# A skewness kernel: another assignment of rows to partitions, a direct store, other load widths and a later split of the closing sums

## Chip, core and metric

The kernel runs on one core of a Trainium2 chip. The metric is the device time of one execution in microseconds (us), as the median of several runs. Each run has a state: slow, if it is over 1.5% above the fastest of the same kernel, else fast. Ratios are the mean time of one kernel's fast runs over that of the other's fast runs of the same rounds, so they are not quite the ratio of the medians that are quoted beside them.

## The reference, cut to what matters

```python
rows, cols = 1024, 8192                      # x is float32, 33.55 MB
mean = np.mean(x, axis=-1, keepdims=True)
std = np.std(x, axis=-1, keepdims=True)
z = (x - mean) / (std + 1e-8)
return np.mean(z ** 3, axis=-1)              # one number for each row
```

With m1, m2, m3 as the means of x, x² and x³ of a row, var = m2 - m1², and the result is (m3 - 3 m1 (var + m1²/3)) · var^(-1.5). So one pass over x is enough, and no order of columns or rows matters to the sums.

## The kernel before

The rows are taken in 8 blocks of 128, one row for each partition. A block comes in by several loads, each a range of columns (a unit). On each unit ScalarE squares and sums, VectorE multiplies the square by x and sums, and TensorE accumulates transposes, which later give m1.

```python
UNITS = [[512, 1024, 2560, 4096], [4096, 4096], [4096, 4096], [4352, 3840],
         [3328, 2816, 2048], [2048] * 4, [1792, 1792, 1664, 1536, 1408],
         [1152, 1152, 1152, 1152, 1024, 896, 896, 512, 256]]     # layout shortened
xv = x.rearrange("(b p) c -> b p c", p=P)
ob = out.rearrange("(b p) -> b p", p=P)
# ...
for k, w in enumerate(widths):
    xt = xpool.tile([P, w], FP, tag="x", name=f"x_{b}_{k}")
    nc.sync.dma_start(out=xt, in_=xv[b, :, c0 : c0 + w])
    c0 += w
    for s, e in _slices(w):
        # ...
        nc.scalar.activation(out=sq, in_=xt[:, s:e], func=AF.Square, scale=s_scale, accum_out=a2)
        nc.vector.scalar_tensor_tensor(out=cube, in0=sq, scalar=1.0, in1=xt[:, s:e],
                                       op0=ALU.mult, op1=ALU.mult, accum_out=a3)
    # ... transposes of xt into tp on TensorE
# ... blocks 0 to 6 closed together, then block 7:
nc.vector.tensor_scalar(out=m3, in0=v3, scalar1=nm1, scalar2=m3, op0=ALU.mult, op1=ALU.add)
nc.vector.tensor_tensor(out=skew[:, L:NB], in0=m3, in1=rr, op=ALU.mult)
nc.tensor.matmul(out=skT_ps, lhsT=skew, rhs=ident, start=True, stop=True, is_transpose=True)
nc.vector.tensor_copy(out=skT, in_=skT_ps)
nc.sync.dma_start(out=ob, in_=skT)
```

Partition p of block b holds row 128b+p. Written with p = 8e+i that is row 128b+8e+i.

## Time and profile before

| what | value | from |
|---|---|---|
| time | 93.59 us, median of 3 runs (93.39 to 94.45) | the runs |
| span of the profiled run | 91.36 us | the trace |
| first packet of a load, last landing | 1.75 us, 84.93 us | the trace's packet and landing records |
| a packet of 16384 B, of 8192 B (median) | 611 ns, 312 ns | the packet records |
| VectorE, ScalarE, TensorE busy | 81%, 76%, 74% | the page |

A packet here is one row's part of one unit: the 5 loads of 16384 B per row show 640 packets, so 128 a load, 8 for each of its 16 landings. The landing records have one time for each engine's share of a load, and a unit is used when the last of the 16 is there (the first unit's is at 3.69 us, ScalarE's first square of it at 3.78). The page's lines, the waits and the timeline are shown and read in the prediction.

### The profile page before, as it was taken

How to read it: one execution, taken by the hardware profiler on the slowest of the kernel's cores; microseconds unless marked ns; L12 is line 12 of the kernel's file. 1: busy time of each engine (PE TensorE's matmuls, PEld its weight loads, DVE VectorE, ACT ScalarE, POOL GpSimd, SP SyncE). 2: the span in 40 equal slices, each digit the busy share in tenths (PEclk: the TensorE clock that was granted, in tenths of full speed). 3: DMA queues.
4: the chain of work that ended last, by engine and by line, in shares of the span. 5: the costliest groups of instructions: out<-in, count | busy, mean ns of one | idle time of the engine just before them, and what ended most of it. 6: DMA issues, size and time to landing. Idle time of an engine off the chain costs nothing. (4 is left out here: it accounts for less than half of the span.)

```text
span 91.4 us, 1437 instructions
## 1 busy us (share of the span) xinstructions
PE 68.0 (74%) x529; PEld 60.6 (66%) x529; DVE 73.9 (81%) x91; ACT 69.1 (76%) x101; POOL 9.4 (10%) x14
## 2 busy tenths in 40 slices
PE   0391898879495949688889897857789798989610
PEld 0360897779494939587879796747678687867500
DVE  0052290898989798978999999998899999999960
ACT  6350927969595959689889999766798899999830
POOL 3000000000000000000000000000000000699820
PEclk9999999999999999999999999999999999999995
DMA  1999999999999999999999999999999999991000
GB/s 43 362 374 440 445 438 409 430 452 430 402 423 452 442 417 434 435 424 399 430 414 404 430 420 420 423 407 422 419 409 423 406 418 408 406 344 74 0 0 2
DMA packets 4486, 33.64 MB, mean 368 GB/s; under 512 B 504, under 2 KB 640, under 8 KB 2560
## 3 DMA queue, kind: packets, MB, share of 16 engines
q1 hardware_dynamic: 4480, 33.56, 88.6%
q8 instruction: 4, 0.07, 0.3%
q14 instruction: 2, 0.02, 0.0%
HBM read 33.55 MB, written 0.00 MB: 367 GB/s over the span
## 5 line engine op out<-in xcount | busy, mean ns | idle before, releaser
L139 DVE SCALAR_TENSOR_TENSOR sq<-sq,x 128x2048 f32<-128x2048 f32 (+11 forms) x39 | 71.5, 1885 | 13.9 <-ACT sq L135 13.9
L145 PE MATMUL tp<-ident,x 128*128 128x128 f32 x512 | 65.2, 285 | 15.3 <-DMA x<-in_x_dram 15.0
L135 ACT ACTIVATE sq<-x 128x2048 f32<-128x2048 f32 (+12 forms) x41 | 62.8, 1534 | 17.4 <-DMA x<-in_x_dram 15.9
L145 PEld LDWEIGHTS tp<-ident,x 128*128 128x128 f32 x512 | 58.7, 147 | 20.5 <-DMA x<-in_x_dram 16.6
L106 POOL TENSOR_TENSOR vara<-m2a,m1sqa 128x7 f32<-128x7 f32 x1 | 1.3, 1294 | 77.1 <-DVE m3a L97 77.1
L135 ACT ACTIVATION_READ_ACCUMULATOR sq<-x 128x1 f32 x41 | 7.6, 186 | 0.0
L116 PEld LDWEIGHTS s1ps<-onesn,tsb 128*128 128x128 f32 x16 | 2.4, 188 | 5.6 <-ACT tsb L115 5.6
L116 PE MATMUL s1ps<-onesn,tsb 128*128 128x1 f32 x16 | 3.1, 260 | 3.7 <-ACT tsb L115 3.7
L139 DVE DVE_READ_ACCUMULATOR sq<-sq,x 128x1 f32 x39 | 3.2, 83 | 0.0
L110 POOL TENSOR_TENSOR rra<-vara,expo 128x7 f32<-128x7 f32 x1 | 2.6, 2624 | 0.0
L115 ACT COPY tsb<-tp 128x128 f32<-128x128 f32 x8 | 2.0, 249 | 0.0
L72 ACT ACT_TABLE_LOAD x1 | 1.3, 1283 | 0.7 <-PEq L190 0.7
L172 PE MATMUL skT_ps<-ident,skew 128*8 128x128 f32 x1 | 0.3, 273 | 2.0 <-DVE skew L169 2.0
L172 PEld LDWEIGHTS skT_ps<-ident,skew 128*8 128x8 f32 x1 | 0.1, 83 | 2.1 <-DVE skew L169 2.1
L107 POOL TENSOR_TENSOR m1sq3a<-m1sq3a,vara 128x7 f32<-128x7 f32 x1 | 1.2, 1202 | 0.1
L139 DVE SCALAR_TENSOR_TENSOR cubes<-sq,x 128x512 f32<-128x512 f32 (+1 forms) x2 | 1.1, 554 | 0.1
L108 POOL TENSOR_TENSOR m1sq3a<-m1sq3a,nm1a 128x7 f32<-128x7 f32 x1 | 1.1, 1150 | 0.0
L109 POOL TENSOR_TENSOR m3a<-m3a,m1sq3a 128x7 f32<-128x7 f32 x1 | 0.9, 935 | 0.1
L111 POOL TENSOR_TENSOR skew<-m3a,rra 128x7 f32<-128x7 f32 x1 | 0.9, 933 | 0.1
L70 DVE MEMSET onesn<- 128x1 f32 x1 | 0.1, 59 | 0.8 <-PEq L190 0.8
L163 POOL TENSOR_TENSOR rrl<-varl,expo 128x1 f32<-128x1 f32 x1 | 0.6, 562 | 0.6 <-ACT varl L161 0.6
L174 DVE COPY skT<-skT_ps 8x128 f32<-8x128 f32 x1 | 0.3, 278 | 0.4 <-PE skT_ps L172 0.4
(25 smaller groups left out, 4.4 us busy)
## 6 DMA issues: line engine op xcount, KB each, us to landing
x<-in_x_dram SPq DMA_DIRECT2D x5, 2048.0 KB, 18.7
x<-in_x_dram SPq DMA_DIRECT2D x5, 1024.0 KB, 24.2
x<-in_x_dram SPq DMA_DIRECT2D x4, 576.0 KB, 9.8
x<-in_x_dram SPq DMA_DIRECT2D x1, 2176.0 KB, 33.8
x<-in_x_dram SPq DMA_DIRECT2D x1, 1920.0 KB, 36.2
x<-in_x_dram SPq DMA_DIRECT2D x2, 896.0 KB, 15.8
x<-in_x_dram SPq DMA_DIRECT2D x1, 1664.0 KB, 33.9
x<-in_x_dram SPq DMA_DIRECT2D x1, 1408.0 KB, 30.3
```

Source lines behind the costliest of these rows:

```text
L72: nc.scalar.activation(out=tiny, in_=onesn, func=AF.Square)
L106: g.tensor_tensor(out=var, in0=m2, in1=m1sq, op=ALU.subtract)
L107: g.tensor_tensor(out=m1sq3, in0=m1sq3, in1=var, op=ALU.add)
L108: g.tensor_tensor(out=m1sq3, in0=m1sq3, in1=nm1, op=ALU.mult)
L109: g.tensor_tensor(out=m3, in0=m3, in1=m1sq3, op=ALU.add)
L110: g.tensor_tensor(out=rr, in0=var, in1=expo, op=ALU.pow)
L111: g.tensor_tensor(out=skew[:, 0:L], in0=m3, in1=rr, op=ALU.mult)
L115: nc.scalar.copy(out=tsb, in_=tp)
L116: nc.tensor.matmul(out=s1ps[:, b : b + 1], lhsT=tsb, rhs=onesn, start=True, stop=True)
L135: nc.scalar.activation(out=sq, in_=xt[:, s:e], func=AF.Square, scale=s_scale, accum_out=a2)
L139: nc.vector.scalar_tensor_tensor(out=cube, in0=sq, scalar=1.0, in1=xt[:, s:e], op0=ALU.mult, op1=ALU.mult, accum_out=a3,)
L145: nc.tensor.matmul(out=tp, lhsT=xt[:, c * P : (c + 1) * P], rhs=ident, start=(k == 0 and c == 0), stop=(c0 == C and c == n - 1), is_transp ...
```

## The change

Its intent: to shorten the time after the last landing. If partition 8e+i holds rows 128i+8e+b for b from 0 to 7, its 8 results lie side by side in the output, and the finished tile can be stored directly, without a transpose and a copy. The m1 term of the last two blocks becomes one more column of the third sums, so that one reduction adds it. Larger first and last units mean fewer loads. The core of the diff (cut):

```diff
 UNITS = [
-    [512, 1024, 2560, 4096],
-    ...
-    [1152, 1152, 1152, 1152, 1024, 896, 896, 512, 256],
+    [4096, 4096],
+    [4096, 4096],
+    [4096, 4096],
+    [4096, 4096],
+    [3584, 2304, 2304],
+    [2304, 2304, 2048, 1536],
+    [1664, 1792, 1920, 1664, 1152],
+    [1024, 1024, 1152, 1280, 1408, 1152, 1152],
 ]
+S1_ACT = {(0, 0): 1024, (1, 0): 1024, (2, 0): 1024}   # column sums on ScalarE, not TensorE
+EARLY = 6                                             # blocks 0 to 5 closed early
...
-    xv = x.rearrange("(b p) c -> b p c", p=P)
-    ob = out.rearrange("(b p) -> b p", p=P)
+    I = P // ENGINES                                  # ENGINES = 16, I = 8
+    xv = x.rearrange("(i e b) c -> b e i c", i=I, e=ENGINES, b=NB)
+    ov = out.rearrange("(i e b) -> e i b", i=I, e=ENGINES, b=NB)
...
-            nc.sync.dma_start(out=xt, in_=xv[b, :, c0 : c0 + w])
+            nc.sync.dma_start(out=xt, in_=xv[b, :, :, c0 : c0 + w])
...
+        yield act(out=s3u[:, b * K + K - 1 : b * K + K], in_=v3, func=AF.Identity, scale=nm1)
...
-    nc.vector.tensor_scalar(out=m3, in0=v3, scalar1=nm1, scalar2=m3, ...)
-    nc.tensor.matmul(out=skT_ps, lhsT=skew, rhs=ident, ..., is_transpose=True)
-    nc.vector.tensor_copy(out=skT, in_=skT_ps)
-    nc.sync.dma_start(out=ob, in_=skT)
+    nc.vector.tensor_reduce(out=num, in_=s3u[:, F * K :]..., axis=X_AXIS, op=ALU.add)
+    nc.vector.tensor_tensor(out=skew[:, F:NB], in0=num, in1=rr, op=ALU.mult)
+    nc.sync.dma_start(out=ov, in_=skew)
```

More of the change, by code (lines that the diff above doesn't have):

```diff
@@ L15 @@
 UNITS = [
-    [512, 1024, 2560, 4096],
     [4096, 4096],
     [4096, 4096],
-    [4352, 3840],
-    [3328, 2816, 2048],
-    [2048, 2048, 2048, 2048],
-    [1792, 1792, 1664, 1536, 1408],
-    [1152, 1152, 1152, 1152, 1024, 896, 896, 512, 256],
+    [4096, 4096],
[4 more added lines that the diff above has]
+    [1024, 1024, 1152, 1280, 1408, 1152, 1152],
 ]
+S1_ACT = {(0, 0): 1024, (1, 0): 1024, (2, 0): 1024}
 SUB_MAX = 2304
@@ L27 @@
 SQ_BUFS = 4
-PSUM_SQ = 2
+EARLY = 6
+ENGINES = 16
 def _slices(w):
@@ L48 @@
     L = NB - 1
+    F = EARLY
     inv_n = 1.0 / float(C)
@@ L52 @@
     assert len(UNITS) == NB and all(sum(u) == C for u in UNITS)
-    xv = x.rearrange("(b p) c -> b p c", p=P)
-    ob = out.rearrange("(b p) -> b p", p=P)
-    n_sub = [sum(len(_slices(w)) for w in u) for u in UNITS]
-    MAXC = max(n_sub[:L])
-    NL = n_sub[L]
+    nw = len(S1_ACT)
+    assert sorted(b for b, _ in S1_ACT) == list(range(nw)) and nw <= F
+    I = P // ENGINES
+    xv = x.rearrange("(i e b) c -> b e i c", i=I, e=ENGINES, b=NB)
+    ov = out.rearrange("(i e b) -> e i b", i=I, e=ENGINES, b=NB)
+    K = max(sum(len(_slices(w)) for w in u) for u in UNITS) + 1
     xpool = ctx.enter_context(tc.tile_pool(name="xp", bufs=X_BUFS))
@@ L65, with small @@
     psum = ctx.enter_context(tc.tile_pool(name="ps", bufs=2, space=bass.MemoryType.PSUM))
-    psq = ctx.enter_context(tc.tile_pool(name="psq", bufs=2, space=bass.MemoryType.PSUM))
     psum1 = ctx.enter_context(tc.tile_pool(name="ps1", bufs=1, space=bass.MemoryType.PSUM))
-    onesn = onep.tile([P, 1], FP, tag="onesn")
+    def small(name, n):
+        return onep.tile([P, n], FP, tag=name, name=name)
+    onesn = small("onesn", 1)
     nc.vector.memset(onesn, inv_n)
-    tiny = onep.tile([P, 1], FP, tag="tiny")
+    tiny = small("tiny", 1)
@@ L72 @@
     nc.scalar.activation(out=tiny, in_=onesn, func=AF.Square)
-    ident = onep.tile([P, P], FP, tag="ident")
+    ident = small("ident", P)
     make_identity(nc, ident)
-    s2u = onep.tile([P, L * MAXC], FP, tag="s2u")
-    s3u = onep.tile([P, L * MAXC], FP, tag="s3u")
+    s2u = small("s2u", NB * K)
+    s3u = small("s3u", NB * K)
     nc.vector.memset(s2u, 0.0)
     nc.vector.memset(s3u, 0.0)
-    s2l = onep.tile([P, NL], FP, tag="s2l")
-    s3l = onep.tile([P, NL], FP, tag="s3l")
-    cubes = onep.tile([P, 512], FP, tag="cubes")
@@ L82 @@
-    junk = onep.tile([P, NL], FP, tag="junk")
-    expo = onep.tile([P, L], FP, tag="expo")
+    s1a = small("s1a", nw)
+    same = small("same", max(S1_ACT.values()))
+    junk = small("junk", K)
+    expo = small("expo", F)
     nc.gpsimd.memset(expo, -1.5)
-    skew = onep.tile([P, NB], FP, tag="skew")
+    skew = small("skew", NB)
     s1ps = psum1.tile([P, NB], FP, tag="s1ps")
-    Tsb = [onep.tile([P, P], FP, tag=f"tsb{i}", name=f"tsb{i}") for i in range(2)]
-    def small(name, n):
-        return onep.tile([P, n], FP, tag=name, name=name)
@@ L93, in finish_first_blocks, with close_first_blocks @@
-    def finish_first_blocks():
-        m2, m3 = small("m2a", L), small("m3a", L)
+    m1a = small("m1a", F)
+    var2 = small("var2", NB - F)
+    Tsb = [small(f"tsb{i}", P) for i in range(2)]
+    def close_first_blocks():
+        m2, m3 = small("m2a", F), small("m3a", F)
         for dst, src in ((m2, s2u), (m3, s3u)):
             nc.vector.tensor_reduce(
-                out=dst, in_=src.rearrange("p (b c) -> p b c", c=MAXC), axis=X_AXIS, op=ALU.add
-            )
-        m1sq, m1sq3, nm1 = small("m1sqa", L), small("m1sq3a", L), small("nm1a", L)
-        nc.scalar.activation(out=m1sq, in_=s1ps[:, 0:L], func=AF.Square)
-        nc.scalar.activation(out=m1sq3, in_=s1ps[:, 0:L], func=AF.Square, scale=third)
-        nc.scalar.activation(out=nm1, in_=s1ps[:, 0:L], func=AF.Copy, scale=-3.0)
+                out=dst, in_=src[:, 0 : F * K].rearrange("p (b c) -> p b c", c=K),
+                axis=X_AXIS, op=ALU.add,
+            )
+        m1sq, m1sq3, nm1 = small("m1sqa", F), small("m1sq3a", F), small("nm1a", F)
+        nc.scalar.copy(out=m1a[:, nw:F], in_=s1ps[:, nw:F])
+        nc.scalar.activation(out=m1sq, in_=m1a, func=AF.Square)
+        nc.scalar.activation(out=m1sq3, in_=m1a, func=AF.Square, scale=third)
+        nc.scalar.activation(out=nm1, in_=m1a, func=AF.Copy, scale=-3.0)
@@ L104, in finish_first_blocks @@
         g = nc.gpsimd
-        var, rr = small("vara", L), small("rra", L)
+        var, rr = small("vara", F), small("rra", F)
         g.tensor_tensor(out=var, in0=m2, in1=m1sq, op=ALU.subtract)
@@ L110, in finish_first_blocks, with close_on_act @@
         g.tensor_tensor(out=rr, in0=var, in1=expo, op=ALU.pow)
-        g.tensor_tensor(out=skew[:, 0:L], in0=m3, in1=rr, op=ALU.mult)
-    def close_block(b, tp):
-        tsb = Tsb[b % 2]
-        nc.scalar.copy(out=tsb, in_=tp)
-        nc.tensor.matmul(out=s1ps[:, b : b + 1], lhsT=tsb, rhs=onesn, start=True, stop=True)
+        g.tensor_tensor(out=skew[:, 0:F], in0=m3, in1=rr, op=ALU.mult)
+    def close_on_act(b):
+        m2, m1sq, nm1, v3 = (small(f"{t}_{b}", 1) for t in ("m2", "m1sq", "nm1", "v3"))
+        p1 = s1ps[:, b : b + 1]
+        var = var2[:, b - F : b - F + 1]
+        act = nc.scalar.activation
+        yield act(out=junk, in_=s2u[:, b * K : b * K + K], func=AF.Copy, accum_out=m2)
+        yield act(out=m1sq, in_=p1, func=AF.Square)
+        yield act(out=var, in_=m1sq, func=AF.Identity, scale=-1.0, bias=m2)
+        yield act(out=nm1, in_=p1, func=AF.Copy, scale=-3.0)
+        yield act(out=v3, in_=m1sq, func=AF.Identity, scale=1.0 / 3.0, bias=var)
+        yield act(
+            out=s3u[:, b * K + K - 1 : b * K + K], in_=v3, func=AF.Identity, scale=nm1
+        )
@@ L118 @@
+    pending = iter(())
     for b, widths in enumerate(UNITS):
-        last = b == L
         tp = psum.tile([P, P], FP, tag="tp", name=f"tp_{b}")
         c0 = 0
-        j = 0
+        j = b * K
         for k, w in enumerate(widths):
+            last_unit = b == L and k == len(widths) - 1
             xt = xpool.tile([P, w], FP, tag="x", name=f"x_{b}_{k}")
-            nc.sync.dma_start(out=xt, in_=xv[b, :, c0 : c0 + w])
+            nc.sync.dma_start(out=xt, in_=xv[b, :, :, c0 : c0 + w])
@@ L126 @@
             c0 += w
             for s, e in _slices(w):
-                i = b * MAXC + j
-                a2 = s2l[:, j : j + 1] if last else s2u[:, i : i + 1]
-                a3 = s3l[:, j : j + 1] if last else s3u[:, i : i + 1]
-                j += 1
-                in_psum = last and k >= len(widths) - PSUM_SQ
-                pool = psq if in_psum else sqpool
-                sq = pool.tile([P, e - s], FP, tag="sq", name=f"sq_{b}_{k}_{s}")
+                if last_unit:
+                    sq = psum1.tile([P, e - s], FP, tag="sqps", name=f"sqps_{s}")
+                else:
+                    sq = sqpool.tile([P, e - s], FP, tag="sq", name=f"sq_{b}_{k}_{s}")
@@ L135 @@
                 nc.scalar.activation(
-                    out=sq, in_=xt[:, s:e], func=AF.Square, scale=s_scale, accum_out=a2
+                    out=sq, in_=xt[:, s:e], func=AF.Square, scale=s_scale,
+                    accum_out=s2u[:, j : j + 1],
                 )
-                cube = cubes[:, 0 : e - s] if in_psum else sq
+                cube = sqpool.tile([P, e - s], FP, tag="sq", name="cube") if last_unit else sq
                 nc.vector.scalar_tensor_tensor(
                     out=cube, in0=sq, scalar=1.0, in1=xt[:, s:e],
-                    op0=ALU.mult, op1=ALU.mult, accum_out=a3,
+                    op0=ALU.mult, op1=ALU.mult, accum_out=s3u[:, j : j + 1],
@@ L142 @@
                 )
-            n = w // P
+                j += 1
+            w_act = S1_ACT.get((b, k), 0)
+            if w_act:
+                nc.scalar.activation(
+                    out=same[:, 0:w_act], in_=xt[:, w - w_act : w], func=AF.Copy,
+                    scale=inv_n, accum_out=s1a[:, b : b + 1],
+                )
+            n = (w - w_act) // P
             for c in range(n):
@@ L149 @@
                 )
-        close_block(b, tp)
-        if b == L - 1:
-            finish_first_blocks()
-    m2, m3 = small("m2l", 1), small("m3l", 1)
-    nc.scalar.activation(out=junk, in_=s2l, func=AF.Copy, accum_out=m2)
-    nc.vector.tensor_reduce(out=m3, in_=s3l, axis=X_AXIS, op=ALU.add)
-    m1sq, var, nm1, v3 = small("m1sql", 1), small("varl", 1), small("nm1l", 1), small("v3l", 1)
-    p1 = s1ps[:, L:NB]
-    nc.scalar.activation(out=m1sq, in_=p1, func=AF.Square)
-    nc.scalar.activation(out=var, in_=m1sq, func=AF.Identity, scale=-1.0, bias=m2)
-    rr = small("rrl", 1)
-    nc.gpsimd.tensor_tensor(out=rr, in0=var, in1=expo[:, 0:1], op=ALU.pow)
-    nc.scalar.activation(out=nm1, in_=p1, func=AF.Copy, scale=-3.0)
-    nc.scalar.activation(out=v3, in_=m1sq, func=AF.Identity, scale=1.0 / 3.0, bias=var)
-    nc.vector.tensor_scalar(
-        out=m3, in0=v3, scalar1=nm1, scalar2=m3, op0=ALU.mult, op1=ALU.add
-    )
-    nc.vector.tensor_tensor(out=skew[:, L:NB], in0=m3, in1=rr, op=ALU.mult)
-    skT_ps = psum1.tile([NB, P], FP, tag="skT")
-    nc.tensor.matmul(out=skT_ps, lhsT=skew, rhs=ident, start=True, stop=True, is_transpose=True)
-    skT = small("skT", P)[0:NB, :]
-    nc.vector.tensor_copy(out=skT, in_=skT_ps)
-    nc.sync.dma_start(out=ob, in_=skT)
+            if k > 0:
+                next(pending, None)
+                next(pending, None)
+        tsb = Tsb[b % 2]
+        nc.scalar.copy(out=tsb, in_=tp)
+        nc.tensor.matmul(out=s1ps[:, b : b + 1], lhsT=tsb, rhs=onesn, start=True, stop=True)
+        if b == F - 2:
+            nc.vector.tensor_tensor(
+                out=m1a[:, 0:nw], in0=s1ps[:, 0:nw], in1=s1a, op=ALU.add
+            )
+        if b == F - 1:
+            close_first_blocks()
+        if b >= F:
+            pending = close_on_act(b)
+    for _ in pending:
+        pass
+    rr = small("rr2", NB - F)
+    nc.gpsimd.tensor_tensor(out=rr, in0=var2, in1=expo[:, 0 : NB - F], op=ALU.pow)
+    num = small("num2", NB - F)
+    nc.vector.tensor_reduce(
+        out=num, in_=s3u[:, F * K :].rearrange("p (b c) -> p b c", c=K), axis=X_AXIS, op=ALU.add
+    )
+    nc.vector.tensor_tensor(out=skew[:, F:NB], in0=num, in1=rr, op=ALU.mult)
+    nc.sync.dma_start(out=ov, in_=skew)
 _INS = ['x']
```

## The prediction

Marked cuts in it are passages on the hardware that no trace or run here shows; one is the whole argument against the first rival, the 4 MiB pitch. No term of the sum is cut: 84.4 + 3.7 + 2.06 + 0.25 = 90.4 us of span, 92.6 us of time.

> **What bounds the kernel now.** I read the page's head first, for shares and the DMA row.
>
> ```profile
> span 91.4 us, 1437 instructions
> PE 68.0 (74%) x529; PEld 60.6 (66%) x529; DVE 73.9 (81%) x91; ACT 69.1 (76%) x101; POOL 9.4 (10%) x14
> ...
> DMA  1999999999999999999999999999999999991000
> GB/s 43 362 374 440 445 438 409 430 452 430 402 423 452 442 417 434 435 424 399 430 414 404 430 420 420 423 407 422 419 409 423 406 418 408 406 344 74 0 0 2
> ```
>
> No engine is above 81%, but the 16 DMA engines are at 90% or more from the second slice to the 36th, at 400 to 450 GB/s. The load of the 33.55 MB sets the pace, and every engine only follows. Next the waits of all engines, to see who follows whom:
>
> ```profile
> ACT sq L135 <- DMA x<-in_x_dram: 15.9, 16, 3.1
> PE tp L145 <- DMA x<-in_x_dram: 15.0, 18, 3.8
> DVE sq L139 <- ACT sq L135: 13.9, 11, 3.5
> ```
>
> ScalarE and TensorE wait for loads, VectorE for ScalarE's squares. So the time splits in two: the stream until the last column has landed, and the tail after that. The trace's landing records (one time for each engine's share of a load) put the last landing at 84.93 us. Its own packets start at 1.75. The tail is 91.36 - 84.93 = 6.43 us, and the timeline of the end shows what is in it:
>
> ```profile
> 84.53 1.09 DVE L139 SCALAR_TENSOR_TENSOR sq<-sq,x 128x896 f32<-128x896 f32 x1
> ...
> 85.55 1.08 DVE L139 SCALAR_TENSOR_TENSOR sq<-sq,x 128x896 f32<-128x896 f32 x1
> ...
> 86.56 0.68 DVE L139 SCALAR_TENSOR_TENSOR cubes<-sq,x 128x512 f32<-128x512 f32 x1
> ...
> 87.34 0.42 DVE L139 SCALAR_TENSOR_TENSOR cubes<-sq,x 128x256 f32<-128x256 f32 x1
> 87.69 0.08 DVE L139 DVE_READ_ACCUMULATOR cubes<-sq,x 128x1 f32 x1
> 87.81 0.16 DVE L157 TENSOR_REDUCE m3l<-s3l 128x1 f32<-128x9 f32 x1
> 88.09 0.28 DVE L166 TENSOR_SCALAR m3l<-v3l,nm1l,m3l 128x1 f32<-128x1 f32 x1
> 88.47 0.16 DVE L169 TENSOR_TENSOR skew<-m3l,rrl 128x1 f32<-128x1 f32 x1
> 89.00 0.28 DVE L174 COPY skT<-skT_ps 8x128 f32<-8x128 f32 x1 [0.37 <-PE skT_ps L172]
> ```
>
> VectorE still has 2.84 us of cubes to do when the last column lands (87.77 - 84.93): the many small last units did not help, as it works through a queue. Then five small steps, 87.81 to 89.28. The store is issued at 89.30 and 2.06 us later the span ends. ScalarE's line beside it, which matters for what follows:
>
> ```profile
> 85.60 0.37 ACT L135 ACTIVATE sq<-x 128x256 f32<-128x256 f32 x1
> ...
> 86.00 0.24 ACT L115 COPY tsb<-tp 128x128 f32<-128x128 f32 x1
> ...
> 86.72 0.17 ACT L160 ACTIVATE m1sql<-s1ps 128x1 f32<-128x1 f32 x1 [0.27 <-PE s1ps L116]
> ...
> 86.92 0.29 ACT L161 ACTIVATE varl<-m1sql,m2l 128x1 f32<-128x1 f32 x1
> 87.25 0.29 ACT L165 ACTIVATE v3l<-m1sql,varl 128x1 f32<-128x1 f32 x1
> ```
>
> It ends at 87.54, 0.55 us before VectorE takes v3l at 88.09. Today it is hidden.
>
> [...]
> [...] a packet of 16384 B takes 611 ns (median), so 16 engines make 429 GB/s. [...]
> [...] The new mapping puts neighbouring partitions 128 rows, that is 4 MiB, apart. Nothing in the trace of before tests it, since its pitch is 32 KiB.
> [...] The new store writes 32 B per partition; the old one 512 B rows. Not testable in this trace either.
> [...] 512 columns take 0.63 us into SBUF at 3.78 and 0.58 us into PSUM at 84.99.
>
> **The change, part by part.**
> Stream. The packet medians of the trace fit 10 ns + 36.8 ps per byte (16384 B 611 ns, 8192 B 312, 4608 B 182, 1024 B 46). One packet is one row of a unit, so each engine has 8 per load. Before has 31 loads, after 27: 32 fewer packets per engine, 32 x 10 ns = 0.32 us less. The bytes are the same. Each load also has end markers and a small gap, and the first packets of 2048 and 4096 B ran longer than their median; for both together I take 0.2 us, a guess at the lower side of 0.6 us of start-up excess. Last landing: 84.93 - 0.5 = 84.4 us. It is set by the slowest engine: in before, the last landing of its 16 is 1.05 us after the fifteenth, since one engine lost about 1 us around 60.9 us, at a fetch of instructions in the trace. I leave that in; it may fall on another engine.
>
> Start. The first unit is now 2 MB instead of 256 KB. Before had its first 4096 columns landed at 9.33; after should have them near 8.5 to 9, so VectorE starts near 10.7 (one 2048-column square, 1.91 + 0.19 us) and not at 4.54. VectorE's work: 65536 columns x 1.04 ns (1152 columns every 1.28 us, less 0.08 for the read) = 68.3, plus 36 reads x 0.08 = 2.9, together 71.2. 10.7 + 71.2 = 81.9, before the stream ends, so the late start is paid from idle time: VectorE does 4096 columns in 4.4 us, the loads take 5.0.
>
> TensorE and ScalarE. The first 20 transposes of the third unit took 4.53 us (0.23 each), the later 32 take 3.7 (0.12). Starting late and slow, TensorE would lag, so 3 x 1024 columns go to ScalarE, 3 x (1.06 + 0.19) = 3.8 us early in the run, where ScalarE has over 0.5 us to spare per 5 us unit. Worth nothing to the end, costs nothing.
>
> Block 6's closing sums now run on ScalarE inside block 7, some 2 us with a wait for TensorE. Its squares of 1152 take 1.20 us against a landing every 1.43 (1.24 ns per column), and 1408 1.40 against 1.75. With widths 1024, 1024, 1152, 1280, 1408 I work out that it has caught up by the fifth unit of the block.
>
> Tail, counted from the last landing T. Squares of 1152 columns start at T + 0.09 (as 80.60 against a landing of 80.52) and end at T + 1.2. VectorE is one unit behind and takes the last from T + 1.55 to T + 2.9 (1.27 + 0.08). So the drain stays what it was, 2.84. After it come the reduction (0.28 to the next start), one multiplication, then the store. The TENSOR_SCALAR, the TensorE transpose and the copy are gone: from 87.81 to 89.30 is 1.49 us before, 0.48 after if nothing else is waited for. That is the intended gain, 1.0 us.
>
> But the m1 term is now a column of the reduction's input, so the reduction waits for ScalarE. The copy of the transposes at T + 1.25 (TensorE needs 9 x 0.127 = 1.14 us); then by before's row the square 0.72 later, var 0.92, v3 1.25, and one more step, 1.58 to 1.87. That is T + 3.12, against VectorE's T + 2.9. The power on GpSimd starts at T + 2.54; one column took 0.56 and seven took 2.62, so two take 0.9, to T + 3.45. The multiplication can start near T + 3.48, the store at T + 3.7. Before it was T + 4.37. Gain 0.67 instead of 1.0.
>
> Store. 128 writes of 32 B over 16 engines instead of 8 rows of 512 B: I add 0.25 us, a guess, to 2.06.
>
> Sum: 84.4 + 3.7 + 2.06 + 0.25 = 90.4 against 91.36, so 0.95 us less. From the median of 93.59: 92.6 us, -1.0%.
>
> **Rivals.**
> The 4 MiB pitch slows the loads. [...] If it holds after all, packets of 16384 B take well over 611 ns and the time grows by many microseconds (100 or more). I give it 6%.
> The stream's end moves by its slowest engine. Four engines were up to 1.3 us late from the first 2 MB on, and instruction fetches hit others by about 1 us. If they fall better, T is near 83.4 and the time 91.6; if worse, 93.6.
> VectorE or ScalarE bounds the end after all: if ScalarE's block 6 sums aren't caught up, or the late start isn't, the last cube ends 0.5 to 1.5 us later, 93 to 94 us. Against it: the slack of 0.6 us per 4096 columns.
> ScalarE's and GpSimd's chain is hidden: then the full 1.0 us comes, 92.3.
>
> **Range and chances.** The middle is 92.6. The slowest engine alone is worth a microsecond either way, the tail's two guesses 0.3 each: 91.3 to 93.7 should hold it 8 times in 10. Faster by over 2% means below 91.7: it needs the better fall of the slow engine and most of the tail, 0.21. Slower by over 2%, above 95.5, needs the pitch or a stall I don't see: 0.06. Within 2%: 0.73.
>
> **What would show it.** Packets of 16384 B at 611 ns (mapping harmless); last landing 84.4 and 16 landings spread by 2 to 3 us; VectorE's first cube near 10.7 and its idle time still laid to ScalarE; the last reduction released by ScalarE and not by VectorE's own cube; the multiplication released by GpSimd; store issued 3.7 us after the last landing and 2.3 us to the end. It is wrong if packets grow, if VectorE never idles after 20 us, or if the store takes over 3 us.

## The result, and the profile after

The changed kernel is correct and takes 163.24 us (median of 4 runs, 162.17 to 166.35), against 93.49 us for the kernel before in the same session. The ratio is 1.746, with a 95% interval of 1.725 to 1.768. The profiled run, at 166.35 us, fell in the slow state; what it shows below is far larger than that, and the fast profiles of the experiments repeat it.

Lines of the page of the changed kernel:

```profile
span 164.6 us, 1368 instructions
...
PE 89.1 (54%) x504; PEld 81.1 (49%) x504; DVE 74.4 (45%) x80; ACT 73.9 (45%) x106; POOL 5.2 (3%) x14
...
DMA  5999999999999999999999999999999999999500
GB/s 139 203 223 203 207 231 207 203 227 207 203 231 203 203 231 203 199 235 203 221 209 209 213 222 215 220 228 229 222 233 230 225 231 242 249 243 234 141 0 1
```

VectorE and ScalarE work about as long as before, 74 us each. The DMA row is as full as before, but the same 90% and more now move 200 to 250 GB/s instead of 400 to 450. A full DMA row says that packets are always under way, not that they move fast: one must read it together with the row below it. The packet records say the same: 16384 B take 1268 ns (median), 8192 B 608, 4096 B 276. About 16 packets are under way at every moment, as many as there are engines (16.05 in the mean between 20 and 60 us, 16.03 before).

The waits of the changed kernel, which answer to those of before:

```profile
DVE sq L154 <- ACT sq L149: 83.5, 25, 14.5
ACT sq L149 <- DMA x<-in_x_dram: 70.9, 23, 11.2
PE tp L167 <- DMA x<-in_x_dram: 67.7, 26, 13.5
```

ScalarE and TensorE now wait for the loads some 70 us each in all, and VectorE 83.5 us for ScalarE's squares. The last landing is at 156.81 us instead of 84.93: 71.9 us of the 73.2 us that the span grew by. So the cause is to be sought in the loads, and the tail, which the change was made for, is a side matter.

### The profile page after: what moved, and what is told of

It is laid out like the page before. It is cut to its first block, busy times and chain, and to the rows that moved or that the text cites. A ratio compares the mean times of both kernels' runs of the same rounds, so it can differ in the third digit from the quotient of the medians.

```text
span 164.6 us, 1368 instructions
## 1 busy us (share of the span) xinstructions
PE 89.1 (54%) x504; PEld 81.1 (49%) x504; DVE 74.4 (45%) x80; ACT 73.9 (45%) x106; POOL 5.2 (3%) x14
## 4 chain that ended last, share of the span: by engine, by line
DMA 52%; PE 20%; another core or an unknown queue 14%; ACT 7%; DVE 2%; issue 2%; SPq 1%; ACTq 0%; DVEq 0%
DMA x<-in_x_dram 52%; PE tp L167 19%; ACT sq L149 6%; DVE sq L154 2%; SPq L142 1%; PE s1ps L177 1%; ACT tsb L176 1%; ACT s3u L130 0%; ACT v L129 0%; ACT var L127 0%; DVE num L191 0%; ACT m1sq L126 0%; DVE skew L194 0%; ACTq L149 0%
## 5 line engine op out<-in xcount | busy, mean ns | idle before, releaser
L167 PE MATMUL tp<-ident,x 128*128 128x128 f32 x488 | 85.8, 352 | 67.9 <-DMA x<-in_x_dram 67.7
L167 PEld LDWEIGHTS tp<-ident,x 128*128 128x128 f32 x488 | 78.5, 187 | 73.7 <-DMA x<-in_x_dram 60.2
L154 DVE SCALAR_TENSOR_TENSOR sq<-sq,x 128x2048 f32<-128x2048 f32 (+9 forms) x35 | 71.9, 2074 | 83.5 <-ACT sq L149 83.5
L149 ACT ACTIVATE sq<-x 128x2048 f32<-128x2048 f32 (+9 forms) x35 | 60.7, 1734 | 73.2 <-DMA x<-in_x_dram 70.9
L149 ACT ACTIVATION_READ_ACCUMULATOR sq<-x 128x1 f32 x35 | 6.5, 186 | 0.0
L161 ACT ACTIVATE same<-x 128x1024 f32<-128x1024 f32 x3 | 3.1, 1042 | 0.0
L154 DVE SCALAR_TENSOR_TENSOR cube<-sqps,x 128x1152 f32<-128x1152 f32 x1 | 1.4, 1358 | 1.1 <-ACT sqps L149 1.1
L115 POOL TENSOR_TENSOR m3a<-m3a,m1sq3a 128x6 f32<-128x6 f32 x1 | 1.7, 1726 | 0.1
L149 ACT ACTIVATE sqps<-x 128x1152 f32<-128x1152 f32 x1 | 1.1, 1136 | 1.2 <-DMA x<-in_x_dram 1.2
L116 POOL TENSOR_TENSOR rra<-vara,expo 128x6 f32<-128x6 f32 x1 | 1.3, 1337 | 0.0
```

The lines of the kernel that those rows point to most:

```text
L115: g.tensor_tensor(out=m3, in0=m3, in1=m1sq3, op=ALU.add)
L116: g.tensor_tensor(out=rr, in0=var, in1=expo, op=ALU.pow)
L161: nc.scalar.activation(out=same[:, 0:w_act], in_=xt[:, w - w_act : w], func=AF.Copy, scale=inv_n, accum_out=s1a[:, b : b + 1],)
L167: nc.tensor.matmul(out=tp, lhsT=xt[:, c * P : (c + 1) * P], rhs=ident, start=(k == 0 and c == 0), stop=(c0 == C and c == n - 1), is_transp ...
```

## The experiments

Theories at the start: A, neighbouring partitions 4 MiB apart in memory meet in the same part of it, so that packets slow down; B, the form of the load's view; C, something else of the change, such as the larger units. All runs below are the changed kernel with one edit, except where the kernel before is named. "Wrong" means that the rows or their order no longer match the reference, while the bytes and packets stay the same.

### Four kernels on the rows

First, the rows of before in the changed kernel:

```diff
-    xv = x.rearrange("(i e b) c -> b e i c", i=I, e=ENGINES, b=NB)
-    ov = out.rearrange("(i e b) -> e i b", i=I, e=ENGINES, b=NB)
+    xv = x.rearrange("(b e i) c -> b e i c", i=I, e=ENGINES, b=NB)
+    ov = out.rearrange("(b e i) -> e i b", i=I, e=ENGINES, b=NB)
```

> The changed kernel with one thing undone: partition 8e+i of block b reads row 128b+8e+i again (pitch 32 KiB from partition to partition), written with the same three-dimensional view; the result goes out in 1024 pieces of 4 B. Theory A (the 4 MiB pitch of the rows slows each packet): packets of 16384 B back from 1268 ns to about 611, last landing near 84.4 us, time 92 to 95 us (the 4 B store may cost 0.5 to 2 us). Theory B (the shape of the view, not the addresses, splits or slows the loads): packets stay near 1268 ns and the time near 163 us. Theory C (something else of the change, such as 16 KB packets from the start, loads the memory worse): also near 163 us.

Measured: correct, 98.57 us (98.46 to 99.17). Packets of 16384 B take 611 ns and the last landing is at 83.63 us. So the loads are whole again, and theory C falls. The rest of the time is the store in pieces of 4 B: issued at 87.30, landed at 95.60, 8.3 us and a much higher price than the 0.5 to 2 us that I had guessed. (The 128 pieces of 32 B of the third kernel below land 1.4 us after the issue, 87.28 to 88.69.) I took B as refuted by this run, since the view is written with the same three dimensions. That was a mistake, as the later runs show: with these rows the dimensions e and i run with one uniform stride (8 rows and 1 row), and the instruction has them merged into one (its loads are recorded as [128,1], those of the changed kernel as [1,128]).

Second, the kernel before with only the rows of its loads changed:

```diff
-    xv = x.rearrange("(b p) c -> b p c", p=P)
+    xv = x.rearrange("(i e b) c -> b e i c", i=8, e=16, b=NB)
...
-            nc.sync.dma_start(out=xt, in_=xv[b, :, c0 : c0 + w])
+            nc.sync.dma_start(out=xt, in_=xv[b, :, :, c0 : c0 + w])
```

> The kernel before with nothing changed but the rows of its loads (128i+8e+b to partition 8e+i of block b); the store is left as it was, so the result comes out in another order, wrong on purpose. Theory A: 155 to 170 us, packets of 16384 B near 1268 ns and of 4608 B near 313 instead of 182. Theory C: within 2% of before.

Measured: 160.85 us (156.24 to 161.88; the profiled run 156.24); wrong. 16384 B take 1242 ns, 4608 B 255 ns instead of 182. So this line alone carries the loss.

Third, another mapping that allows the direct store:

```diff
-    xv = x.rearrange("(i e b) c -> b e i c", i=I, e=ENGINES, b=NB)
-    ov = out.rearrange("(i e b) -> e i b", i=I, e=ENGINES, b=NB)
+    xv = x.rearrange("(e i b) c -> b e i c", i=I, e=ENGINES, b=NB)
+    ov = out.rearrange("(e i b) -> e i b", i=I, e=ENGINES, b=NB)
```

> The changed kernel with rows 8p+b on partition p: it still stores 32 B per partition directly, but the pitch from partition to partition is 256 KiB and the engines' groups of 8 partitions lie 2 MiB apart. If the large pitch between neighbouring partitions is what costs (A1): near full speed, 92 to 94 us, packets of 16384 B at 611 to 650 ns. If it is the distance between the rows that the 16 engines read at the same moment that costs, once it is 2 MiB or more (A2): clearly slower, 110 to 163 us.

Measured: correct, 91.54 us (91.44 to 91.60) against 92.45 of before, ratio 0.988 (0.982 to 0.994). 16384 B take 611 ns. It is 1.2% faster than the kernel before: the interval excludes 1. Its DMA row on its page:

```profile
DMA  4899999999999999999999999999999999994000
GB/s 117 321 431 438 431 445 416 438 438 423 431 431 423 423 431 431 423 431 429 415 409 418 415 435 419 414 422 424 399 421 412 410 415 415 409 415 170 0 0 2
```

The row is as full as in the changed kernel, and the row below it is twice as high. By theory A this fitted too: 256 KiB instead of 4 MiB.

Fourth, the addresses moved off the exact multiple of 4 MiB:

```diff
-            nc.sync.dma_start(out=xt, in_=xv[b, :, :, c0 : c0 + w])
+            src = bass.AP(tensor=x.tensor, offset=b * C + c0 + 7 * 1024,
+                          ap=[[8 * C, 16], [128 * C - 1024, 8], [1, w]])
+            nc.sync.dma_start(out=xt, in_=src)
```

> The changed kernel with its rows, but each of an engine's 8 partitions starts 4 KiB further to the left in its row than the one before, so the pitch is 4 MiB less 4 KiB; the columns spill into the next row, so the result is wrong on purpose; bytes and packets are the same. If exact multiples of 4 MiB meet in the same part of the memory (A, aliasing): near full speed, 92 to 95 us, packets of 16384 B at 611 to 700 ns. If distance as such costs (far rows, whatever their low bits): still near 163 us.

Measured: 162.44 us (161.41 to 164.47), wrong, 16384 B in 1259 ns. No help at all. Theory A in its simplest form falls; what is left of it is distance as such, or collisions coarser than 4 KiB.

### Four kernels on the step and on the engines

The step of an engine from one of its rows to the next was set to 127 and to 64 rows, again as an explicit view:

```diff
+            src = bass.AP(tensor=x.tensor, offset=(b) * C + c0, ap=[[8 * C, 16], [127 * C, 8], [1, w]])
```

> The changed kernel with partition 8e+i of block b on row 127i+8e+b instead of 128i+8e+b, so an engine steps 127 rows (4064 KiB) from one of its packets to the next; some rows are read twice and others not, so the result is wrong on purpose, the bytes and packets are the same. The 4 KiB stagger did not help. If it is the distance of the step as such (D): still 155 to 165 us, 16384 B packets near 1268 ns. If the rows collide because their addresses agree in the bits below 4 MiB, only coarser than 4 KiB (P, parts of the memory chosen by bits from 32 KiB up): near full speed, 90 to 97 us, 611 to 650 ns.

Measured: 163.27 us (162.39 to 164.90), wrong, 16384 B in 1268 ns: the same as with 128 rows. So theory P of the expectation, a collision of rows whose addresses agree in the bits from 32 KiB up, falls too.

```diff
+            src = bass.AP(tensor=x.tensor, offset=(b) * C + c0, ap=[[8 * C, 16], [64 * C, 8], [1, w]])
```

> The changed kernel with row 64i+8e+b: the step is 2 MiB, half of the changed kernel's, a power of two still (result wrong on purpose, some rows read twice). Theory P says that the step need not be exactly 4 MiB: slow if the bit of 2 MiB plays no part either, fast if it does; theory D says in between or slow, since it is still a long step. Full speed (90 to 94 us) would put the border between 2 and 4 MiB, 163 us between 256 KiB (the run with rows 8p+b was at full speed) and 2 MiB[...].

Measured: 162.53 us (160.08 to 166.19, two of the four runs slow), wrong, 16384 B in 1271 ns. Half the step makes no difference. A cost that does not depend on the step is a poor fit to any theory of the step.

Then two kernels that were meant to use 8 of the 16 engines. The first cuts each load of the changed kernel in two:

```diff
+            for h in range(2):
+                src = bass.AP(tensor=x.tensor, offset=(b + 64 * h) * C + c0,
+                              ap=[[8 * C, 8], [128 * C, 8], [1, w]])
+                nc.sync.dma_start(out=xt[64 * h : 64 * h + 64, :], in_=src)
```

> The changed kernel with each load cut into two of 64 partitions whose outermost dimension is 8, so that only 8 of the 16 engines carry data, with the changed kernel's rows (correct result). If each engine is slowed by its own long step (per engine): packets of 16384 B stay near 1268 ns and the time doubles to about 320 us. If the memory behind gives only about 210 GB/s for such rows (shared limit): 8 engines alone can use 8 x 26.8 = 214 GB/s, so packets go back to 611 to 700 ns and the time stays near 160 to 175 us.

Measured: correct, 244.55 and 279.71 us in its two runs (the second slow). 8.03 packets are under way in the mean, 8 landings a load, so 8 engines it is. Their packets of 16384 B take 1178 ns. A shared limit of 210 GB/s is out, since for the first 26 slices 8 engines together got only 84 to 130 GB/s:

```profile
DMA  3455445454545545545455545454555555555520
GB/s 84 111 119 113 116 113 119 116 116 113 124 111 127 124 113 130 119 127 122 122 122 124 130 120 130 125 149 163 193 211 211 202 208 202 198 210 212 208 88 1
```

The last slices are another matter, and explain why the run took 245 us and not 320. The packets of 9216 B fall from a median of 453 ns (before 165 us) to 347 (after 172 us), and from then on this same view is at full speed: 8192 B take 309 ns and 4608 B 178, against 608 and 313 in the changed kernel. So neither the view nor its rows slow every packet down. The end of the part on the prediction comes back to this.

The second, the control, differs in the rows:

```diff
-                src = bass.AP(tensor=x.tensor, offset=(b + 64 * h) * C + c0,
-                              ap=[[8 * C, 8], [128 * C, 8], [1, w]])
+                src = bass.AP(tensor=x.tensor, offset=(128 * b + 64 * h) * C + c0,
+                              ap=[[8 * C, 8], [1 * C, 8], [1, w]])
```

> The control for the run before: the same cut into 8 engines with the rows of the kernel before (128b+8e+i). Every theory: packets of 16384 B at 611 ns and about 155 to 165 us, since 8 engines at 26.8 GB/s need 157 us for 33.55 MB. If it is far from that, the cut doesn't do what I think and the pair says nothing. The result is written to the changed kernel's places and is wrong on purpose.

Measured: 163.37 and 165.23 us, wrong. The time is as expected and yet the expectation failed: 16.03 packets are under way, not 8, and each of 16384 B takes 1264 ns. Here all rows of a block lie side by side, as in the kernel before, and still the packets are slow:

```profile
DMA  5999999999999999999999999999999999999700
GB/s 136 209 209 225 209 209 225 209 201 225 213 205 221 213 205 209 221 217 205 223 211 199 220 223 219 221 223 224 221 241 227 236 231 239 246 248 242 188 0 1
```

Distance in memory cannot be the cause here. What the run has of its own is that each load goes to 64 partitions only, 0 to 63 or 64 to 127.

### The new theory

In the control, loads to 64 partitions moved 201 to 225 GB/s in slices 2 to 20, about half of what those to 128 did in the kernel before, with as many packets under way (16.03 in both) and the same rows. So what a load writes counts, and not only what it reads. No run here shows which engine writes which partition.

The trace records the destination of each load instruction, and there is the difference that the source text hides. It lists two counts for the partitions written; the plain loads have theirs in the first place, the others in the second (first loads of 16384 B per row):

```
kernel before, rows 128b+8e+i, rows 8p+b:        dst_num_elem=[128,1] dst_elem_size=16384
changed kernel, steps of 127 rows, of 64 rows:   dst_num_elem=[1,128] dst_elem_size=16384
two halves, rows of the change:                  dst_num_elem=[1,64]  dst_elem_size=16384
two halves, rows of before:                      dst_num_elem=[64,1]  dst_elem_size=16384
```

Where e and i together run with one stride, the load is recorded as a plain one over 128 partitions. Where they don't, it is recorded in the other form. Theory S, my inference: a load in the other form is dealt out by the outer dimension, so engine e gets the neighbours 8e to 8e+7, and which partitions are written at the same time sets the rate. For the first half there is the count of packets: an outer dimension written as 8 gave 8.03 under way where it stayed, and 16.03 where it merged with the next. For the second there are the times of 16384 B:

| load | packets under way | 16384 B |
|---|---|---|
| 128 partitions, [128,1] (kernel before) | 16.03 | 611 ns |
| 128 partitions, [1,128] (changed kernel) | 16.05 | 1268 ns |
| 64 partitions, [64,1] (two halves, rows of before) | 16.03 | 1264 ns |
| 64 partitions, [1,64] (two halves, rows of the change) | 8.03 | 1178 ns |

The last three come out at about half the speed per engine. By what mechanism is not shown.

### Two kernels to test it, and two on what is left

Near rows in a view that can't be merged:

```diff
+            src = bass.AP(tensor=x.tensor, offset=(110 * b) * C + c0, ap=[[9 * C, 16], [C, 8], [1, w]])
```

> New theory S: what counts is not how far the rows lie apart but whether the load's view is one uniform stride over the 128 partitions. The views of the two fast runs (128b+8e+i, 8p+b) are; those of all slow runs with 16 engines (steps of 128, 127, 64 rows beside a step of 8) are not. Where it is not, each engine would get 8 neighbouring partitions 8e to 8e+7 at a time[...]. This run is the changed kernel with row 110b+9e+i: steps of 32 KiB, engines' groups 288 KiB apart, all near, but not one uniform stride (result wrong on purpose). S: slow, 155 to 165 us, 16384 B packets 1200 to 1280 ns. Long steps being the cause (A, D): full speed, 92 to 95 us, 611 ns.

Measured: 162.98 us (161.32 to 165.02), ratio 1.737 (1.723 to 1.750), wrong, 16384 B in 1266 ns. The rows are near and the loss is whole: long steps are not needed for it.

Long steps with 4 neighbouring partitions for each engine, by theory S, instead of 8:

```diff
+            for g in range(4):
+                row = b + 64 * (g // 2) + 512 * (g % 2)
+                src = bass.AP(tensor=x.tensor, offset=row * C + c0,
+                              ap=[[8 * C, 8], [128 * C, 4], [1, w]])
+                nc.sync.dma_start(out=xt[32 * g : 32 * g + 32, :], in_=src)
```

> The changed kernel with each load cut into four of 32 partitions with view 8 x 4: 8 engines, each on 4 neighbouring partitions[...]; the 4 MiB steps and the set of rows stay, and the view is not one stride (result wrong on purpose). S[...]: packets of 16384 B at 611 to 650 ns, though the steps are long, and about 160 to 175 us for 8 engines at 26.8 GB/s. Long steps (per engine), or the view's shape as such: about 1180 ns as in the run with two halves of 64 partitions, 245 to 280 us.

Measured: 172.80 and 173.43 us, wrong. 8.03 packets under way, 16384 B in 611 ns. The two lines of its page, beside those of the two halves above:

```profile
DMA  2555555555555555554544554545555555545300
GB/s 84 215 215 218 215 215 218 215 215 211 218 218 215 215 215 215 215 215 211 218 205 207 216 211 209 220 208 207 211 211 213 209 209 209 196 196 200 161 1 1
```

Both kernels use 8 engines and steps of 4 MiB, and both views keep two dimensions (recorded as [1,64] and [1,32]). With 8 neighbouring partitions for each engine, by theory S, it is 111 to 130 GB/s in slices 2 to 26, with 4 it is 215, which is 8 engines at their full 26.8 GB/s (16384 B in 611 ns). So neither the steps nor the unmerged form as such slow a packet down; with 16 packets under way, steps of 4 MiB were only seen in slow loads. By elimination, what is left is which partitions the engines write at the same time. Why 4 neighbours for each go at full speed here and 8 do not is not shown.

The kernel before with rows 8p+b:

```diff
-    xv = x.rearrange("(b p) c -> b p c", p=P)
+    xv = x.rearrange("(p b) c -> b p c", p=P)
```

> The kernel before with only the rows of its loads changed to 8p+b, one uniform stride of 256 KiB (result in another order, wrong on purpose). S: the same as before within 1%, against 160.85 us with the rows of the change in the same kernel: then the whole loss hangs on the form of the mapping and none on renumbering the rows as such. If scattering the rows costs something of its own: 1 to 5% slower.

Measured: 94.43 us (91.95 to 95.37), wrong; only two of its six runs count as fast, with the ratio 0.995 (0.984 to 1.005), and 16384 B take 611 ns. The runs scatter more than those of the other kernels at full speed, so a small cost of its own of up to 2% is not excluded. A loss of 70% is.

Last, rows 8p+b with the end of the kernel before:

```diff
-    nc.sync.dma_start(out=ov, in_=skew)
+    nc.tensor.matmul(out=skT_ps, lhsT=skew, rhs=ident, start=True, stop=True, is_transpose=True)
+    nc.vector.tensor_copy(out=skT, in_=skT_ps)
+    nc.sync.dma_start(out=out.rearrange("(b p) -> b p", p=P), in_=skT)
```

> The changed kernel with rows 8p+b and, instead of the direct store, the end of the kernel before: TensorE transpose, copy, store of 8 rows of 512 B (result in another order, wrong on purpose). The direct store drops 0.6 us of steps (88.64 to 89.30 in before) but takes 2.5 us from issue to the end instead of 2.06. If both are right: 0.1 to 0.3 us slower than the run with rows 8p+b (91.54), so 0.985 to 0.992 of before. If the direct store is worth its full 0.6: 92.1 us, 0.995.

Measured: 92.17 us (92.03 to 92.39), ratio 0.991 (0.987 to 0.995), wrong. Against 0.988 for the direct store that is about 0.3 us, and the intervals overlap. In the traces the store is issued 0.65 us later (87.93 instead of 87.28), and the span ends 2.31 us after the issue instead of 2.50. So the direct store is worth some 0.5 us of the span, of which the runs can only show that it is small.

## Why the prediction was wrong, and what of it held

The step that failed stands in the part on the stream: the last landing at 84.4 us, from packet times of 10 ns + 36.8 ps per byte carried over to the changed kernel, with "The bytes are the same". The bytes were; the time of a packet was not. 16384 B went from 611 to 1268 ns, and the last landing came at 156.81 us.

The first rival had the size right ("100 or more", 611 ns no longer holding) and 6% of the chance. But it named the wrong place, the 4 MiB pitch in memory. Steps of 64 and 127 rows cost the same as 128, the 4 KiB stagger changed nothing, near rows in an unmerged view were as slow, and 4 MiB steps ran at full speed (611 ns) in loads to 32 partitions with 8 packets under way. The argument that I set against the rival rested on which partitions and rows each engine has; that was my assumption, which no trace or run shows, so it is cut, and the 6% stand without their reason. I looked only at the source side of the load and never asked which partitions are written together. One reading was also loose, without weight for the result: slices 2, 3 and 36 of the kernel before are at 362, 374 and 344 GB/s, not 400 to 450.

The rest of the working can be tested on the run with rows 8p+b, which is the change without the accident. The end of its timeline, with ScalarE's, VectorE's and GpSimd's lines and the store:

```profile
83.63 1.14 ACT L149 ACTIVATE sqps<-x 128x1152 f32<-128x1152 f32 x1
...
84.89 0.27 ACT L176 COPY tsb<-tp 128x128 f32<-128x128 f32 x1
...
85.31 1.35 DVE L154 SCALAR_TENSOR_TENSOR cube<-sqps,x 128x1152 f32<-128x1152 f32 x1
...
86.21 0.70 POOL L189 TENSOR_TENSOR rr<-var,expo 128x2 f32<-128x2 f32 x1 [7.69 <-ACT var L127]
86.49 0.29 ACT L130 ACTIVATE s3u<-v,nm 128x1 f32<-128x1 f32 x1
...
86.82 0.17 DVE L191 TENSOR_REDUCE num<-s3u 128x2 f32<-128x16 f32 x1
87.09 0.16 DVE L194 TENSOR_TENSOR skew<-num,rr 128x2 f32<-128x2 f32 x1
87.28 0.35 SPq L195 DMA_DIRECT2D out_dram<-skew  x1
```

Its last landing is T = 83.61.

- Last landing: predicted 84.4, measured 83.61, before 84.93. The fewer packets and the better start were worked out as 0.5 us of these 1.32. The 84.93 is from an earlier session; in the rounds of this run the kernel before took 92.45 us instead of 93.59, so part of the rest can be the session's. The one engine that came 1.05 us after all others in before is missing here: the last two landings are 83.56 and 83.61, and all 16 spread over 2.1 us. The prediction had left this open ("If they fall better, T is near 83.4 and the time 91.6").
- First cube on VectorE: predicted near 10.7, measured 10.35. The late start cost nothing: by the end VectorE had caught up, as the next point shows.
- Last cube: predicted to end at T + 2.9, measured 86.66 = T + 3.05, against T + 2.84 in the kernel before.
- The m1 column: predicted at T + 3.12, measured 86.78 = T + 3.17. It comes after the last cube, so the reduction starts at 86.82 behind ScalarE's step, as said, though only by about 0.1 us.
- The power on GpSimd: predicted 0.9 us for two columns and an end at T + 3.45; it took 0.70 and ended at T + 3.30. The multiplication at 87.09 did not wait for it but for the reduction, which ended at 86.99. This part was wrong, by 0.15 us; that the multiplication still came at T + 3.48, as forecast, is luck.
- Store: issued at T + 3.67 (predicted 3.7); 2.50 us to the end (predicted 2.31).
- Sum: 92.6 from 93.59 was -1.0%; this run measured -1.2% against before of its own rounds. The sum agrees better than its parts. From the last landing to the end it is 6.17 us, against 6.43 before: the tail, which the change was made for, gives 0.26 us where 0.42 (0.67 less 0.25 for the store) was predicted, since the store takes back 0.44 of the 0.70 gained before it. The rest of the gain is the earlier last landing. It came at 83.61 to 83.63 us in all three profiled runs of the changed kernel with loads that merge; of the kernel before with its own rows there is one profile, so how much of the difference would repeat stays open.

In the changed kernel itself the tail is longer, 7.75 us from the last landing to the end. Its last 9 transposes took 2.18 us, at a granted clock of 0.50, against 1.20 us at 1.00 in the run with rows 8p+b, and ScalarE's copy waited 0.98 us for them; the reduction waited for ScalarE there too:

```profile
159.07 0.27 ACT L176 COPY tsb<-tp 128x128 f32<-128x128 f32 x1 [0.98 <-PE tp L167]
...
161.20 0.17 DVE L191 TENSOR_REDUCE num<-s3u 128x2 f32<-128x16 f32 x1 [1.71 <-ACT s3u L130]
...
161.66 0.59 SPq L195 DMA_DIRECT2D out_dram<-skew  x1
```

What stays open: the packet records have no engine number, so that engine e writes partitions 8e to 8e+7 is inferred from the number of packets under way and from the speeds, not seen; nor is it shown how partitions that are written together slow each other down. Also open is why the rate creeps up late in the slow runs (249 GB/s in the changed kernel; up to 212 with 8 engines in two halves, which is their full speed). In the two halves the 8 landings of one load lie within 1.3 us early on (21.2 to 22.5) and within 5.3 us late (156.8 to 162.1), so the engines fall out of step. Whether that raises the rate was not tested, and it is not the whole of it: a spread of 4.9 us (91.4 to 96.3) is there already while the rate is still some 120 GB/s.

## What to carry to other kernels

When a load's source view is changed, look at whether its dimensions still merge into one stride over all 128 partitions, since here 128-partition loads recorded as [128,1] moved 16384 B in 611 ns and those recorded as [1,128] in 1242 to 1271; a mapping that merges (here rows 8p+b) gave the direct store without the loss. A DMA row that is full everywhere says nothing of speed (it was full here at 611 and at 1268 ns): read it with the GB/s row and with the time of one packet of a known size. And run the control of an experiment even if it seems idle: here the control that "should" have been fast showed that the theory was wrong.
